# A decoder layer on one core: the first norm's weight from the common load, the first row block in two transfers, four warm-up products in place of five

## The chip, the core and the metric

The kernel runs on one core of one Trainium2 chip. A core has a matrix engine (TensorE, PE in the profile, with its weight loads shown apart as PEld), three engines for elementwise work (VectorE = DVE, ScalarE = ACT, GpSimd = POOL), an engine that mostly starts transfers (SyncE = SP), and 16 DMA engines that all queues share. TensorE multiplies operands that lie in SBUF and writes to PSUM; the input tensors lie in HBM and come in by DMA. The metric is the device time of one execution in microseconds (us); lower is better.

## The reference

One layer of a decoder trunk over 256 tokens of width 1024, in float32:

```python
n = _rmsnorm(x, norm_mix_g)                    # x * rsqrt(mean(x*x) + EPS) * g
z = n @ w_in                                   # conv a, conv gate, q, k, v, index q/k/w, two gates
y_conv = _conformer_conv(c_a, c_g, ...)        # a * sigmoid(gate), 31 taps, layer norm, silu, w_conv_out
y_attn = _dsa_attention(q, k, v, qi, ki, wi) @ w_attn_out
h = x + (g_conv * y_conv + g_attn * y_attn) @ w_mix_out
h = h + _cross_attention(_rmsnorm(h, norm_x_g), _rmsnorm(mem, norm_mem_g), wx_q, wx_kv, wx_o)
h = h + square(relu(_rmsnorm(h, norm_ffn_g) @ w_ff1)) @ w_ff2
return _rmsnorm(h, norm_final_g)
```

The change touches the first line only: how `x` and `norm_mix_g` reach the chip, and what TensorE does until they are there.

## The kernel before

The order of the work is written out by hand (`tc.manual_schedule()`): each engine runs its instructions in the order in which the code issues them, and waits at an instruction for the semaphores that this instruction needs. Weights come as chunks of 1 MB (`wst`, called `raw0`, `raw1`, ... in the order of `STREAM`); the function `load(parts)` starts one chunk from SP, in so many transfers. A weight is split on the chip into a high and a low float32r part (`hi` on ACT, `lo` on DVE), and a product with the normed input (`n_p`, also split in two) is done in three parts.

The first chunk, `raw0` (key `("conv", 0)`, in `WHOLE`), is different: it isn't split but used as plain float32 and multiplied with `xg`, which is `x` transposed and multiplied by the norm's weight `g`, before the norm's root is known. Its two halves are the gate (`ps_conv00`, named `ps_first` in the code) and the value (`ps_conv01`) of the first 128 channels. All of this is the start of the program:

- Lines 501 to 513, transfers: `g_first` (128 x 8 numbers, 4 KB) is started from ACT's queue; the two row blocks of `x` (128 rows x 1024 columns, 512 KB each, into the tile `x_rm`) from SP's queue; `vec`, the load of all small vectors (36 KB, among them `g_mix`, the same numbers as `g_first`), from POOL's queue. Then SP starts `raw0` and `raw1` in two transfers each, `raw2` in one, `cw` (the taps of the convolution) and `raw3`.
- Lines 514 to 533: DVE makes a tile of zeros, POOL an identity matrix, ACT loads its function table, and TensorE runs the warm-up products (`ps_warm`) on the zeros; their result is not used.
- Lines 562 to 587: TensorE transposes the 2 x 8 blocks of 128 x 128 of `x_rm` into four PSUM tiles `pt_n` (row block 0 first, columns 0 to 7, then row block 1). ACT squares row block 0 and half of row block 1 and sums them, DVE squares the other half, POOL raises the mean to the power -1/2 (`rs_n`). ACT (six columns) and DVE (two) write `xg` = `pt_n` times the weight.
- Lines 590 to 609: TensorE starts the products of `raw0` with `xg` for two columns (`first_products(range(2))`), spreads `rs_n` over the partitions (`ps_rsb_n`), and goes on with the products; meanwhile DVE and ACT make `n_p`.

Each DMA has a semaphore out of a ring of eight for the transfers of SP and ACT (`DMAHW0` to `DMAHW7`, handed out in the order in which the code starts the transfers); before the ring comes round, the next transfer with the same semaphore waits for the one before it. `vec` has `DMASW0`, of POOL's own ring.

Of the kernel before, what the change touches and what calls it, by code (L numbers as in the profile page):

```python
# [8 lines left out]
F32 = mybir.dt.float32  # L9
F32R = mybir.dt.float32r  # L10
BF16 = mybir.dt.bfloat16
AF = mybir.ActivationFunctionType
ALU = mybir.AluOpType
# [3 lines left out]
P = 128  # L17
D = 1024
S = 256
KT = D // P  # L20
# [101 lines left out]
def block_kernel(ctx, tc, x, xt, mem, memt, wst, wki, vecs, convw, gout, out):  # L122
    nc = tc.nc
    ctx.enter_context(tc.manual_schedule())
    pe = Counted(nc.tensor, pe_price)
    dve = Counted(nc.vector, dve_price)
    act = nc.scalar.activation

    cst = ctx.enter_context(tc.tile_pool(name="cst", bufs=1))
# [8 lines left out]
    def t8(name, dt=F32, shape=(P, KT, S)):  # L138
        return big.tile(list(shape), dt, tag="t8", bufs=12, name=name)
# [19 lines left out]
    def ps_aux(name):  # L159
        return bank("aux", 2, name)  # L160
# [337 lines left out]
        return lambda ct, ps: copy_out(dst[:, ct, :], ps)  # L498


    g_first = cst.tile([P, KT], F32, name="g_first")
    nc.scalar.dma_start(g_first, vecs[:, 5 * KT : 6 * KT])
    x_rm = t8("x_rm", F32, (P, 2, D))
    for rb in range(2):
        nc.sync.dma_start(x_rm[:, rb, :], x[rb * P : (rb + 1) * P, :])
    vec = cst.tile([P, 72], F32, name="vec")
    nc.gpsimd.dma_start(vec, vecs)
    bgc, bga, cvb, lng, lnb, g_mix, g_mem, g_x, g_ffn = (vec[:, 8 * j : 8 * j + 8] for j in range(9))
# [20 lines left out]
    nc.scalar.activation(half, half, AF.Sigmoid, bias=0.0, scale=0.0)  # L529
    nc.gpsimd.memset(half, -0.5)  # L530
    ps = ps_aux("ps_warm")
    for j in range(5):
        nc.tensor.matmul(ps, zero_r[:, :P], zero_r, start=True, stop=True)


# [30 lines left out]
    xg = t8("xg")  # L566
# [15 lines left out]
    for kt in range(KT):  # L582
        src = ptn[kt // 2][:, (kt % 2) * S : (kt % 2) * S + S]
        if kt in (4, 6):
            dve.tensor_scalar(xg[:, kt, :], src, g_first[:, kt : kt + 1], None, ALU.mult)
        else:
            act(xg[:, kt, :], src, AF.Copy, scale=g_first[:, kt : kt + 1])


    first = whole["conv", 0]  # L590
# [903 lines left out]
    for c in range(JOINED):  # L1494
        hidden.append(Hidden(c + 2))
        x, later = hidden[c], hidden[c + 2]
# [135 lines left out]
```

## Time and profile before

| | us |
|---|---|
| median of 3 runs | 497.66 |
| lowest, highest run | 497.27, 502.79 |
| the profiled execution | 497.16 |
| its span, from the first to the last instruction | 495.0 |
| TensorE (PE) busy | 487.3 |
| VectorE (DVE) busy | 460.5 |
| ScalarE (ACT) busy | 378.4 |
| GpSimd (POOL) busy | 50.6 |

The span is what the trace covers; 497.16 - 495.0 = 2.16 us of the same execution lie outside it. TensorE's line is nearly full from the second 40th of the span to the 39th, so what a stage costs is what it does to TensorE's start, its gaps and its end. The part of the trace that the change touches is the first 8 us of 495; in the timeline's rows the first number is the start in us from the start of the span, the second the duration of the whole group, and the bracket names the idle time ahead of it and what ended it.

### The profile page before, as it was taken

The numbers are of one execution on the slowest core, as the hardware profiler recorded it, in microseconds if no ns is written. First come the engines' busy times: TensorE is split into PE (matmuls) and PEld (weight loads), VectorE is DVE, ScalarE is ACT, GpSimd is POOL, SyncE is SP. The second block draws the span as 40 slices with busy tenths as digits, with TensorE's granted clock in tenths as the row PEclk, the third lists the DMA queues.
The fourth block names the chain that finished last, engine by engine and source line by source line (L and its number), as shares of the span: only waits on it lengthen the run. The fifth ranks groups of instructions, "written<-read, shape, count | busy, mean of one in ns | idle before, by whom it ended". The sixth has DMA issues, their size and how long they took to land.

```text
span 495.0 us, 7793 instructions
## 1 busy us (share of the span) xinstructions
PE 487.3 (98%) x2832; PEld 429.2 (87%) x2832; DVE 460.5 (93%) x828; ACT 378.4 (76%) x678; POOL 50.6 (10%) x67
## 2 busy tenths in 40 slices
PE   8999999999999999999999999999999999999995
PEld 7888888888888889888889999988998888888884
DVE  4999999999999989989988987899999999999986
ACT  5778879999887786767846558687777878888852
POOL 2002212221111211000000000000010101121000
PEclk9999999999999999999999999999999999999999
DMA  8958676989887977354645552866979879999802
GB/s 318 354 215 276 180 190 198 304 245 253 277 219 223 246 176 213 115 171 175 250 169 183 209 204 87 290 189 138 253 274 292 237 242 262 294 333 314 256 9 85
DMA packets 33430, 110.36 MB, mean 223 GB/s; under 512 B 11104, under 2 KB 13408, under 8 KB 24432
## 3 DMA queue, kind: packets, MB, share of 16 engines
q1 hardware_dynamic: 24416, 93.03, 54.4%
q0 software_dynamic: 8688, 16.64, 17.2%
q8 instruction: 22, 0.36, 0.3%
q10 hardware_dynamic: 288, 0.20, 0.1%
q14 instruction: 16, 0.13, 0.1%
HBM read 99.29 MB, written 1.05 MB: 203 GB/s over the span
## 4 chain that ended last, share of the span: by engine, by line
PE 97%; DVE 1%; issue 0%; ACT 0%; DVEq 0%
PE ps_f L87 18%; PE ps_p L87 15%; PE ps_conv L87 9%; PE ps_co L87 5%; PE ps_mix L87 5%; PE ps_ao L87 5%; PE ps_k L87 5%; PE ps_ga L87 5%; PE ps_gc L87 5%; PE ps_q L87 5%; PE ps_v L87 4%; PE ps_xo L87 3%; PE ps_xq L87 2%; PE ps_xk L87 2%; PE ps_qi L87 2%; PE ps_xv L87 2%
## 5 line engine op out<-in xcount | busy, mean ns | idle before, releaser
L87 DVE TENSOR_TENSOR lo<-raw,hi 128x1024 fp32r<-128x1024 f32 x133 | 161.3, 1215 | 2.5 <-ACT hi L315 2.2
L315 ACT ACTIVATE hi<-raw 128x1024 fp32r<-128x1024 f32 x133 | 138.5, 1048 | 6.2 <-DMA raw<-in_wst_dram 6.1
L87 PE MATMUL ps_f<-ff_p,hi 128*128 128x512 f32 (+1 forms) x320 | 72.4, 347 | 0.0
L87 PEld LDWEIGHTS ps_f<-ff_p,hi 128*128 128x128 f32 x320 | 56.2, 189 | 8.2 <-ACT ft L1344 0.3
L87 DVE SCALAR_TENSOR_TENSOR acc<-u,cw,acc 128x241 f32<-128x241 f32 (+23 forms) x142 | 58.5, 465 | 0.1
L87 PE MATMUL ps_f<-ff_p,lo 128*128 128x256 f32 x256 | 46.8, 282 | 0.0
L87 PEld LDWEIGHTS ps_f<-ff_p,lo 128*128 128x128 f32 x256 | 39.3, 191 | 1.8
L715 POOL DMA_DIRECT2D acc<-products x25 | 21.7, 880 | 124.2 <-ACT products L714 59.5
L87 PE MATMUL ps_conv<-n_p,hi 128*128 128x512 f32 x112 | 29.2, 397 | 0.0
L87 PEld LDWEIGHTS ps_conv<-n_p,hi 128*128 128x128 f32 x112 | 20.4, 188 | 4.4 <-issue 0.3
L714 ACT ACTIVATE products<-u,cw 128x243 f32<-128x243 f32 (+19 forms) x50 | 22.1, 492 | 0.0
L293 ACT ACTIVATE inner<-sums 128x1024 fp32r<-128x1024 f32 x13 | 13.8, 1060 | 10.5 <-DVE sums L87 10.5
L87 DVE TENSOR_TENSOR ft<-ft 128x128 f32<-128x128 f32 (+2 forms) x49 | 19.4, 397 | 1.1 <-ACT ft L1344 0.6
L683 ACT ACTIVATE ring<-u,cw 128x236 f32<-128x236 f32 (+10 forms) x44 | 20.2, 480 | 0.0
L87 PE MATMUL ps_p<-outer,fs 128*128 128x512 f32 x78 | 20.1, 393 | 0.0
L87 PE MATMUL ps_v<-hi,n_p 128*128 128x512 f32 x64 | 19.9, 389 | 0.0
L87 PE MATMUL ps_p<-inner,fs 128*128 128x512 f32 x78 | 19.8, 389 | 0.0
L87 PE MATMUL ps_co<-u_p,hi 128*128 128x512 f32 (+1 forms) x80 | 19.3, 350 | 0.0
L87 PE MATMUL ps_mix<-mix_p,hi 128*128 128x512 f32 (+1 forms) x80 | 19.2, 349 | 0.0
L87 PE MATMUL ps_k<-n_p,hi 128*128 128x512 f32 x64 | 17.4, 403 | 0.0
L87 PE MATMUL ps_q<-n_p,hi 128*128 128x512 f32 x64 | 17.3, 402 | 0.0
L87 PEld LDWEIGHTS ps_p<-inner,fs 128*128 128x128 f32 x78 | 14.6, 188 | 3.0
(445 smaller groups left out, 1215.0 us busy)
## 6 DMA issues: line engine op xcount, KB each, us to landing
raw<-in_wst_dram SPq DMA_DIRECT2D x67, 1024.0 KB, 5.7
raw<-in_wst_dram SPq DMA_DIRECT2D x28, 512.0 KB, 6.7
sums<-in_wst_dram POOLq DMA_DIRECT2D x15, 512.0 KB, 8.0
acc<-products POOLq DMA_DIRECT2D x25, 256.0 KB, 5.5
x_rm<-in_x_dram SPq DMA_DIRECT2D x2, 512.0 KB, 4.0
mem_rm<-in_mem_dram SPq DMA_DIRECT2D x1, 1024.0 KB, 7.6
mem_t<-in_memt_dram SPq DMA_DIRECT2D x1, 1024.0 KB, 9.6
h_t<-in_xt_dram SPq DMA_DIRECT2D x1, 1024.0 KB, 7.0
```

The source lines that it names most:

```text
L87: return fn(*args, **kwargs)
L293: act(hi, src, AF.Copy)
L315: act(hi, raw[:, ns], AF.Copy)
L683: act(dst[:, t, :], u[:, 4 * g + t, : S - s], AF.Copy, scale=cw[:, 4 * g + t, TAPS - 1 - s : TAPS - s])
L714: act(prod[:, a, s:], u[:, t, : S - s], AF.Copy, scale=cw[:, t, TAPS - 1 - s : TAPS - s])
L715: nc.gpsimd.dma_start(acc[:, ts, :], prod, accum_op=ALU.add)
```

## The change

`g_first` and its transfer go away, and `xg` is made with `g_mix`, a slice of `vec`. Row block 0 of `x` comes in two transfers, columns 0 to 511 and 512 to 1023; row block 1 in one, as before. One of the five warm-up products is left out. Nothing that is computed changes.

```diff
-    g_first = cst.tile([P, KT], F32, name="g_first")
-    nc.scalar.dma_start(g_first, vecs[:, 5 * KT : 6 * KT])
     x_rm = t8("x_rm", F32, (P, 2, D))
-    for rb in range(2):
-        nc.sync.dma_start(x_rm[:, rb, :], x[rb * P : (rb + 1) * P, :])
+    for rb, cols in ((0, slice(0, 512)), (0, slice(512, D)), (1, slice(0, D))):
+        nc.sync.dma_start(x_rm[:, rb, cols], x[rb * P : (rb + 1) * P, cols])
     vec = cst.tile([P, 72], F32, name="vec")
     nc.gpsimd.dma_start(vec, vecs)
...
     ps = ps_aux("ps_warm")
-    for j in range(5):
+    for j in range(4):
         nc.tensor.matmul(ps, zero_r[:, :P], zero_r, start=True, stop=True)
...
         if kt in (4, 6):
-            dve.tensor_scalar(xg[:, kt, :], src, g_first[:, kt : kt + 1], None, ALU.mult)
+            dve.tensor_scalar(xg[:, kt, :], src, g_mix[:, kt : kt + 1], None, ALU.mult)
         else:
-            act(xg[:, kt, :], src, AF.Copy, scale=g_first[:, kt : kt + 1])
+            act(xg[:, kt, :], src, AF.Copy, scale=g_mix[:, kt : kt + 1])
```

The instructions keep their order on every engine; what moves is what each waits for. On TensorE, at the start of the program, before the change (a row is one instruction or several alike; in brackets the semaphores that it waits for):

```order
L533 MATMUL ps_warm<-zero_r 128x512 x4
L87 MATMUL pt_n_128<-ident,x_rm 128x128 [waits DMAHW1_49,Pool_49]
L87 MATMUL pt_n_128<-ident,x_rm 128x128
L87 MATMUL pt_n_129<-ident,x_rm 128x128 x2
L87 MATMUL pt_n_130<-ident,x_rm 128x128 x2
L87 MATMUL pt_n_131<-ident,x_rm 128x128 x2
L87 MATMUL pt_n_128<-ident,x_rm 128x128 [waits DMAHW2_49]
```

And after it, at the same place:

```order
L531 MATMUL ps_warm<-zero_r 128x512 x3
L87 MATMUL pt_n_126<-ident,x_rm 128x128 [waits DMAHW0_49,Pool_49]
L87 MATMUL pt_n_126<-ident,x_rm 128x128
L87 MATMUL pt_n_127<-ident,x_rm 128x128 x2
L87 MATMUL pt_n_128<-ident,x_rm 128x128 [waits DMAHW1_49]
L87 MATMUL pt_n_128<-ident,x_rm 128x128
L87 MATMUL pt_n_129<-ident,x_rm 128x128 x2
L87 MATMUL pt_n_126<-ident,x_rm 128x128 [waits DMAHW2_49]
```

The first four transposes now wait for the first half of row block 0 alone, the fifth for the second half, the ninth for row block 1 as before; the first product of `raw0` still waits for that chunk's first half (`DMAHW3`) and for `xg`.

On SP, the transfers before the change:

```order
L505 DMA x_rm<-in_x_dram 128x1024 x2
L184 DMA raw_89<-in_wst_dram 128x1024 x2
L184 DMA raw_92<-in_wst_dram 128x1024 x2
L184 DMA raw_95<-in_wst_dram 128x2048
L512 DMA cw<-in_convw_dram 128x248 [waits DMAHW0_49]
L184 DMA raw_98<-in_wst_dram 128x2048 [waits DMAHW1_49]
```

And after it:

```order
L503 DMA x_rm<-in_x_dram 128x512 x2
L503 DMA x_rm<-in_x_dram 128x1024
L184 DMA raw_88<-in_wst_dram 128x1024 x2
L184 DMA raw_91<-in_wst_dram 128x1024 x2
L184 DMA raw_94<-in_wst_dram 128x2048
L510 DMA cw<-in_convw_dram 128x248 [waits DMAHW0_49]
L184 DMA raw_97<-in_wst_dram 128x2048 [waits DMAHW1_49]
```

SP starts one transfer more ahead of all the weights. `cw` waited for `g_first` (`DMAHW0` before) and now waits for the first half of row block 0; `raw3` waited for row block 0 and now waits for its second half.

On ACT, before the change:

```order
L502 DMA g_first<-in_vecs_dram 128x8
L529 ACT_TABLE_LOAD
L529 ACTIVATE half<-half 128x2 [waits Pool_49]
L570 ACTIVATE junk_full,ss_n<-x_rm 128x1024 [waits DMAHW1_49]
L576 ACTIVATE junk_half,ss_n<-x_rm 128x512 [waits DMAHW2_49]
L587 ACTIVATE xg<-pt_n_128,g_first 128x256 [waits DMAHW0_49,PE_49]
```

And after it:

```order
L527 ACT_TABLE_LOAD
L527 ACTIVATE half<-half 128x2 [waits Pool_49]
L568 ACTIVATE junk_full,ss_n<-x_rm 128x1024 [waits DMAHW1_49,DMAHW0_49]
L574 ACTIVATE junk_half,ss_n<-x_rm 128x512 [waits DMAHW2_49]
L585 ACTIVATE xg<-pt_n_126,vec 128x256 [waits DMASW0_49,PE_49]
```

The start of `g_first`'s transfer is gone from ACT, and the first `xg` waits for `vec`, POOL's transfer, in the place of `g_first`.

## The prediction, made before the changed kernel ran

> **What bounds the kernel now.** I read the page first: the engines' busy time and the chain that ended last.
>
> ```profile
> PE 487.3 (98%) x2832; PEld 429.2 (87%) x2832; DVE 460.5 (93%) x828; ACT 378.4 (76%) x678; POOL 50.6 (10%) x67
> ...
> PE 97%; DVE 1%; issue 0%; ACT 0%; DVEq 0%
> ```
>
> TensorE is the bound: 487.3 of 495.0 us, and 97% of the chain. The change can move the end only by moving TensorE's work near the start. So the second view is the chain over the first 20 us (start, duration, what):
>
> ```profile
> 1.43 0.44 DVE zero_r L517
> ...
> 1.91 2.50 PE ps_warm L533 x5
> 4.41 3.62 PE pt_n L87 x16
> 8.03 0.90 PE ps_conv L87 x4
> 8.94 0.22 PE ps_rsb_n L87 x2
> 9.15 10.98 PE ps_conv L87 x57
> ```
>
> This reads as if TensorE were never without work after 1.91 us: warm-up, transposes, products. By it one warm-up product less, half a us of the 2.50, would be a gain of that half. But a chain names what came last by the profile, and a busy bar can end just when a transfer lands. So the third view is the DMA issues of short stretches, which give for one transfer the time from its start to its landing (last column, us), and the fourth SP's timeline with those starts.
>
> ```profile
> x_rm<-in_x_dram SPq DMA_DIRECT2D x1, 512.0 KB, 3.5
> ...
> x_rm<-in_x_dram SPq DMA_DIRECT2D x1, 512.0 KB, 4.4
> ...
> raw<-in_wst_dram SPq DMA_DIRECT2D x1, 512.0 KB, 6.0
> ...
> vec<-in_vecs_dram POOLq DMA_DIRECT2D x1, 36.0 KB, 4.6
> ```
>
> ```profile
> 0.74 0.86 SPq L505 DMA_DIRECT2D x_rm<-in_x_dram  x2
> 1.18 0.42 SPq L505 DMA_DIRECT2D x_rm<-in_x_dram  x1
> 1.28 0.71 POOL L507 DMA_DIRECT2D vec<-in_vecs_dram  x1 [0.83 <-POOLq L1623]
> 1.64 2.49 SPq L184 DMA_DIRECT2D raw<-in_wst_dram  x5
> 4.50 0.33 SPq L512 DMA_DIRECT2D cw<-in_convw_dram  x1
> ```
>
> Row block 0 landed at 0.74 + 3.5 = 4.24 us, row block 1 at 1.18 + 4.4 = 5.58, `vec` at 1.28 + 4.6 = 5.88, the first half of `raw0` at 1.64 + 6.0 = 7.64. Against these stands TensorE's timeline:
>
> ```profile
> 3.78 0.63 PE L533 MATMUL ps_warm<-zero_r 128*128 128x512 f32 x1
> 4.37 0.72 PEld L87 LDWEIGHTS pt_n<-ident,x_rm 128*128 128x128 f32 x4 [0.68 <-issue]
> 4.40 3.63 PE L87 MATMUL pt_n<-ident,x_rm 128*128 128x128 f32 x16
> ...
> 7.42 0.23 PEld L87 LDWEIGHTS pt_n<-ident,x_rm 128*128 128x128 f32 x1
> 7.76 0.23 PEld L87 LDWEIGHTS ps_conv<-xg,raw 128*128 128x128 f32 x1
> ```
>
> Two things are to be seen. The first transpose loads at 4.37, 0.13 us after row block 0 landed, so it waited for the row block, not for the last warm-up product. And the first product of `raw0` loads at 7.76, 0.12 us after that chunk's first half landed at 7.64. The transposes stand (3.63 - 0.42) / 15 = 0.214 us apart (0.42 is one of them), so the next instruction could have loaded at 7.42 + 0.21 = 7.63. TensorE's readiness and the chunk's landing meet within 0.02 us. From there on the products follow each other, and the chain shows nothing but TensorE: **the landing of the first half of `raw0` is the second floor under everything behind it**, and making TensorE ready sooner can't lift it.
>
> **The change, part by part.**
>
> *One warm-up product less.* TensorE is free for the first transpose at 3.78, where the fifth product started, instead of at the fifth's end; five products started within 3.78 - 1.91 us, 0.47 apart.
>
> *The row block in two.* When does the first half land? The busy time by stretch shows what the DMA engines moved (last column, GB/s):
>
> ```profile
> 1.70:2.30 0.60, 0.39 (x1) 0.39 (x2) 0.16 (x1) 0.60 (x1) 0.53 (x3) 1.00 0.91 205
> 2.30:2.70 0.40, 0.40 (x2) 0.30 (x2) 0.00 (x0) 0.19 (x2) 0.40 (x3) 1.00 0.13 51
> 2.70:3.30 0.60, 0.60 (x3) 0.47 (x2) 0.00 (x0) 0.17 (x1) 0.23 (x4) 1.00 0.89 351
> 3.30:3.90 0.60, 0.60 (x3) 0.33 (x1) 0.00 (x0) 0.00 (x0) 0.00 (x0) 1.00 1.11 421
> ...
> 138.60:139.00 0.40, 0.40 (x3) 0.33 (x2) 0.40 (x1) 0.40 (x1) 0.40 (x1) 1.00 0.00 0
> ```
>
> 0.6 us at 205, 0.4 at 51 and 0.6 at 351 GB/s are 0.12 + 0.02 + 0.21 = 0.35 MB by 3.30. Half a block, 0.26 MB, is through at 3.04; the whole, 0.52 MB, at 3.70, and it landed 0.54 later. So the first half should land near 3.04 + 0.54 = 3.6, ahead of 3.78. The transposes then start at about 3.8, 0.57 us sooner. Four of them take 0.85; the second half, due at about 4.3, is there.
>
> Row block 1 is next. Eight transposes end at 3.8 + 1.71 = 5.51, but the block lands at 5.58, and with the 0.11 us from landing to load (0.13 and 0.12 above) the ninth loads at 5.69. Before, it loaded at 7.42 - 7 x 0.214 = 5.92. Of 0.57 us are left 0.23. The transposes end at 5.69 + 1.71 = 7.40, and the first product waits for `raw0` until 7.64 + 0.11 = 7.75, as before. Nothing is left. What is late next is thus the weight transfer.
>
> *Do the landings move?* The bytes stay. The two terms come from packets, in the DMA rows of three stretches of 0.30 us (queue, packets, MB, share of 16 engines):
>
> ```profile
> q1 hardware_dynamic: 31, 0.13, 102.7%
> q10 hardware_dynamic: 29, 0.00, 5.4%
> ...
> q1 hardware_dynamic: 59, 0.12, 104.4%
> ```
>
> A 4 KB packet took 1.027 x 16 x 0.30 / 31 = 0.159 us, a 2 KB one (59 of them, in the output's stage) 0.085, one of `g_first` 0.009. Row block 0 in 2 KB rows costs each engine 8 x (2 x 0.085 - 0.159) = 0.09 us more; without `g_first`, 128 packets and 16 for its semaphore, each engine saves 9 x 0.009 = 0.08. They cancel: 7.64 stays.
>
> Both ends: at the low end, the pause at 2.30 to 2.70 (51 GB/s) comes from `g_first`'s packets and goes with them, which would bring the stream forward by 0.4 x (400 - 51) / 400 = 0.35, with the 0.08 altogether 0.43 us. I don't take it, because the last row of that fence shows the same pause, at 0 GB/s, 0.6 us after a transfer began at 138 us, with no small transfer beside it. At the high end, SP's extra start (0.42 us, the row at 1.18) delays each later start and each landing in full: +0.42 and +0.09, 0.5 us. I don't take it either: time to landing grows from 3.5 to 4.4 to 6.0 along the queue, so the transfers wait behind bytes, not for their start. I take 0.
>
> *`vec` for `g_first`.* It lands at 5.88. The first `xg` is wanted before the product at 7.75, and takes 0.48:
>
> ```profile
> 6.81 1.57 ACT L587 ACTIVATE xg<-pt_n,g_first 128x256 f32<-128x256 f32 x4 [0.44 <-PE pt_n L87]
> 6.89 0.72 POOL L538 TENSOR_TENSOR rs_n<-ss_n,half 128x2 f32<-128x2 f32 x1 [3.84 <-DVE ss_n L87]
> ```
>
> Four `xg` take 1.57 us, or 0.39 apart; even if ACT began only at 7.27 the first product would not wait, so the cover is 7.27 - 5.88 = 1.39 us. Beyond it each us costs one. The two `xg` of DVE and the power (`rs_n`, ready at 7.61 and used at 8.56 or so) come later still.
>
> *The queues.* ACT loses one start, ahead of its table load, which nobody waits for. `cw` started at 4.50; SP now reaches it at 1.64 + 2.49 + 0.42 = 4.55, when its semaphore and that of `raw3` behind it have gone up (by about 4.3). Both transfers stand behind the 4 MB of `x` and three chunks, so 0.05 us costs nothing.
>
> *The sum:* 0 for the end, with -0.43 and +0.5 as its bounds. The profiled execution, 497.16 us (span 495.0 and 2.16 around it), is 0.50 below the median of 497.66.
>
> **The clock.** TensorE ran at half its clock there, which the page's clock line doesn't show. The same kind of transpose, before and after about 7.8 us (min/median/max ns):
>
> ```profile
> L87 PEld LDWEIGHTS pt_n<-ident,x_rm x16: 183/231/231, 4.4 to 7.4; 128*128 128x128 f32 x16
> L87 PE MATMUL pt_n<-ident,x_rm x16: 404/421/447, 4.4 to 7.6; 128*128 128x128 f32 x16
> ...
> L87 PEld LDWEIGHTS ps_rsb_n<-ident,rs_n x2: 137/137/137, 8.6 to 8.8; 128*128 128x128 f32 x2
> L87 PE MATMUL ps_rsb_n<-ident,rs_n x2: 272/272/273, 8.8 to 8.9; 128*128 128x128 f32 x2
> ```
>
> Two of them stand 0.214 us apart before and start 0.11 apart after (0.22 us of chain for two). So a saving at half clock is worth half if the clock rises at a fixed time. It also means that what makes the clock rise matters. The Trainium skill, "TensorE: Matmul & The Clock Gate", Part 4, says that transposes don't count as busy for the clock; Part 1 says it rises after about 3.4 us of sustained work. By the first, the change removes a fifth of what counts. The trace leans against it: between the last warm-up product and 7.8 us there were 16 transposes and nothing else, and the clock rose right then.
>
> **The rivals.**
>
> *A, the forecast:* the weight transfer holds the first product at 7.75. Chance 0.70. The runs lie at 497.27 and 497.66, the profiled one at 497.16; the middle between the median 497.66 and their mean 497.36 is 497.5.
>
> *B, the start-up pause goes with `g_first`:* the earlier start of TensorE then finds its data, up to -0.43: 497.07 from 497.5. For it: small packets stand between all large ones in the second stretch. Against it: the pause at 138.6 us. Chance 0.10.
>
> *C, the clock rises later.* TensorE has about 0.2 us of holes at the ninth transpose and 0.3 at the first product, and one product less. If only products count, the missing 0.47 us is made up by products at half clock: +0.2. If the rise is put off by as long as the half-clock stretch lasted (1.91 to 7.8, 5.9 us), the products of that time take twice as long: +2.95. The middle is +1.6, or 499.1. Against it: what was said of the transposes. Chance 0.10. By the page's window alone, 3.4 us at half clock, the estimate would be +1.7.
>
> *D, the later starts reach the landings:* +0.5, or 498.0, by the high end above. Chance 0.05.
>
> *E, slower by `vec`:* one place, the wait of the first `xg`. It decides from a landing at 7.27 on. POOL's loads in the full stream take longer than 4.6 us:
>
> ```profile
> sums<-in_wst_dram POOLq DMA_DIRECT2D x15, 512.0 KB, 8.0
> ```
>
> With 8.0, `vec` would land at 9.28 and the first product load near 9.8, 2.0 us later: 499.5. Against it: the same transfer at the same time was there at 5.88. Chance 0.05. C, D and E are the cases that end slower than before; none by 2%, which here is 10 us.
>
> **How the numbers follow.** 497.5 us is A. Below, B's end at half chance and A's own spread of runs (0.35 to either side of 497.5) reach 496.9. Above, D and the lower half of C reach 498.6. Left out are C's upper half (0.05), E (0.05) and a median that falls on a disturbed run like 502.79 (0.05 or so): together under 0.2. So 496.9 to 498.6. About 2% is what a measurement of this kernel is held to tell from no change; no case reaches it: faster 0.01, same 0.97, slower 0.02.
>
> **What would show it.** Right: first transpose near 3.8 instead of 4.37, ninth near 5.7 instead of 5.92, a hole of 0.3 us and then the first `ps_conv` load at 7.75 +- 0.1, `ps_rsb_n` behind it at the short 137 ns, `raw`'s first landing at 7.64 (5.6 us after a start near 2.06), span 495.0 +- 0.5. Wrong: that load below 7.5 (B), above 8.1 with the landing (D) or with `vec` (E), or `ps_rsb_n` and the first products at 231 ns and over (C).

## The result: 0.7% slower, and the profile after

| | before | after |
|---|---|---|
| median of 22 runs, us | 497.22 | 500.98 |
| lowest, highest run | 496.92, 502.79 | 498.68, 502.22 |
| the profiled execution | 497.16 | 502.22 |
| its span | 495.0 | 500.1 |

The ratio of the times is 1.0071, with a 95% interval of 1.0057 to 1.0084: a loss of 3.8 us by the medians, under 2%, but outside the range that was predicted. The profiled execution of after is the slowest of its 22, 5.06 us above the profiled one of before; what follows is read from it, and a median execution loses less.

The page of after, busy time and chain shares by engine, stands against the two lines that the prediction began with:

```profile
PE 489.1 (98%) x2831; PEld 430.3 (86%) x2831; DVE 460.7 (92%) x828; ACT 379.4 (76%) x678; POOL 50.8 (10%) x67
...
PE 96%; DMA 2%; DVE 1%; issue 0%; SPq 0%; ACT 0%; DVEq 0%
```

TensorE is still the bound, but a DMA now holds 2% of the chain, where none stood before. The chain over the first 22 us (start, duration, what) says which:

```profile
1.64 0.43 SPq L503
2.07 0.04 issue
2.11 7.83 DMA raw<-in_wst_dram
9.95 0.14 issue
10.08 2.05 PE ps_conv L87 x4
12.13 0.43 PE ps_rsb_n L87 x2
12.56 9.56 PE ps_conv L87 x35
```

SP starts three pieces of `x`, so `raw0` starts at 2.11 and not at 1.64, and its first half lands at 9.95 and not at 7.64. The landing is 2.31 us late for a start that is 0.47 late. The DMA issues of after, the first two from the stretch 1.50 to 2.00 us and the last two from 2.00 to 2.40 (last column: us from start to landing):

```profile
x_rm<-in_x_dram SPq DMA_DIRECT2D x1, 256.0 KB, 3.2
vec<-in_vecs_dram POOLq DMA_DIRECT2D x1, 36.0 KB, 5.9
...
x_rm<-in_x_dram SPq DMA_DIRECT2D x1, 512.0 KB, 6.8
raw<-in_wst_dram SPq DMA_DIRECT2D x1, 512.0 KB, 7.8
```

The second half of row block 0 started at 1.18 and landed at about 4.3; row block 1 started at 1.64 and landed at 8.4, 2.8 us later than before (5.58). What TensorE did meanwhile, its timeline and its waits (us in total, times, longest):

```profile
2.50 1.48 PE L531 MATMUL ps_warm<-zero_r 128*128 128x512 f32 x3
3.78 1.91 PE L87 MATMUL pt_n<-ident,x_rm 128*128 128x128 f32 x8
8.44 0.77 PE L87 MATMUL pt_n<-ident,x_rm 128*128 128x128 f32 x5 [2.74 <-DMA x_rm<-in_x_dram]
```

```profile
PE pt_n L87 <- DMA x_rm<-in_x_dram: 2.7, 1, 2.7
...
PE ps_conv L87 <- DMA raw<-in_wst_dram: 0.6, 1, 0.6
```

The first eight transposes run as forecast, from 3.78 on; then TensorE stands idle for 2.74 us until row block 1 is there. The chain names `raw0` alone, because it follows the landing that came last; but row block 1 by itself already holds the transposes until 8.44 + 1.10 = 9.54 (1.10 us for all eight), so both late landings delay the first product.

The clock is the other half. Stretches of after (busy time of each engine, then PEclk, DMA share, GB/s), and the second kind of row the prediction asked for, the weight loads of `ps_rsb_n`:

```profile
6.10:9.30 3.20, 0.86 (x8) 0.86 (x8) 0.70 (x2) 0.89 (x3) 0.00 (x0) 1.00 0.87 309
9.50:16.20 6.70, 6.15 (x17) 4.88 (x17) 4.37 (x10) 3.94 (x10) 0.98 (x2) 0.50 1.02 418
16.30:20.00 3.70, 3.70 (x19) 3.26 (x18) 3.62 (x6) 3.70 (x6) 0.00 (x0) 1.00 0.33 137
```

```profile
L87 PEld LDWEIGHTS ps_rsb_n<-ident,rs_n x2: 231/231/231, 11.5 to 11.9; 128*128 128x128 f32 x2
```

231 ns instead of 137: half the clock. The trace's record of the granted clock has it rise at 6.03, fall at 9.44 and rise again at 16.27, after steps of 3.41 and 6.83 us. Before, it rose at 7.88 and stayed. So the products from 10.08 to 16.27 ran at half clock, which costs about 6.19 / 2 = 3.1 us; the first product was 10.08 - 7.84 = 2.24 us late. Together 5.3, and the first product with `n_p` came at 20.15 instead of 14.85, 5.3 later. That accounts for the difference of the two spans, 5.1.

Last, the transfers. The stretch of the start-up pause in after, and a later one, and below the later one in before:

```profile
2.30:2.70 0.40, 0.40 (x2) 0.30 (x2) 0.00 (x0) 0.04 (x1) 0.40 (x3) 1.00 1.05 394
3.20:6.80 3.60, 2.49 (x10) 1.75 (x9) 0.00 (x0) 1.15 (x2) 0.00 (x0) 1.00 0.68 181
```

```profile
3.20:6.80 3.60, 3.60 (x15) 2.82 (x15) 0.86 (x3) 1.87 (x4) 0.00 (x0) 1.00 1.02 351
```

The pause at 2.3 us (51 GB/s before) is gone, but from 3.2 to 6.8 the engines moved 181 GB/s instead of 351. For each of these transfers the trace marks 16 arrivals, as many as there are DMA engines; call each a share. The transfer has landed with the last one. The arrivals of the first half of `raw0` (us, sorted):

```
before  7.10 7.11 7.12 7.14 7.15 7.16 7.25 7.26 7.27 7.30 7.32 7.37 7.53 7.54 7.58 7.65
after   7.05 7.18 7.22 7.25 7.48 7.56 7.64 8.51 9.64 9.66 9.76 9.77 9.80 9.88 9.91 9.95
```

Seven shares of after came about as early as before, one was held up by about 1 us and eight by more than 2: the shares have come apart.

### The profile page after: what moved, and what is told of

The parts are those of the page before. It is cut to its first block, busy times and chain, and to the rows that moved or that the text cites. A ratio compares the mean times of both kernels' runs of the same rounds, so it can differ in the third digit from the quotient of the medians.

```text
span 500.1 us, 7792 instructions
## 1 busy us (share of the span) xinstructions
PE 489.1 (98%) x2831; PEld 430.3 (86%) x2831; DVE 460.7 (92%) x828; ACT 379.4 (76%) x678; POOL 50.8 (10%) x67
## 4 chain that ended last, share of the span: by engine, by line
PE 96%; DMA 2%; DVE 1%; issue 0%; SPq 0%; ACT 0%; DVEq 0%
PE ps_f L87 18%; PE ps_p L87 15%; PE ps_conv L87 10%; PE ps_co L87 5%; PE ps_mix L87 4%; PE ps_ao L87 4%; PE ps_k L87 4%; PE ps_ga L87 4%; PE ps_gc L87 4%; PE ps_q L87 4%; PE ps_v L87 4%; PE ps_xo L87 3%; PE ps_xq L87 2%; PE ps_xk L87 2%; PE ps_qi L87 2%; PE ps_xv L87 2%
## 5 line engine op out<-in xcount | busy, mean ns | idle before, releaser
L293 ACT ACTIVATE inner<-sums 128x1024 fp32r<-128x1024 f32 x13 | 13.8, 1061 | 11.0 <-DVE sums L87 10.9
```

The source lines that it names most:

```text
L293: act(hi, src, AF.Copy)
```

## The experiments

Two questions stand behind the loss: what disturbs the transfers, and what TensorE's hole costs. For the first there were several theories, tried in turn, which bear letters in the expectations. S: the third transfer of `x` itself makes row block 1 late. C: one warm-up product less lowers the clock. V: POOL's `vec`, now the first reader of `vecs`, collides with row block 1. P: the 2 KB pieces. T: the first access to the weights' tensor costs a pause. N: a transfer lands out of proportion late when SP starts it later. Q: a later start costs only its own length. The kernel before ran beside each, with medians of 497.2 or so.

| run | median us | ratio, 95% interval | `raw0` starts | its first half lands | packets over 0.6 us |
|---|---|---|---|---|---|
| after | 500.98 | 1.0071 [1.0057, 1.0084] | 2.11 | 9.95 | 6 |
| g_first kept | 500.35 | 1.0085 [1.0049, 1.0120] | 2.11 | 8.81 | 2 |
| split alone | 500.12 | 1.0052 [1.0037, 1.0067] | 2.12 | 8.61 | 5 |
| g_first's removal alone | 498.34 | 1.0028 [1.0013, 1.0044] | 1.65 | 8.97 | 8 |
| four warm-up products alone | 497.29 | 1.0036 [0.9994, 1.0078] | 1.64 | 7.66 | 0 |
| hole filled | 498.69 | 1.0032 [1.0019, 1.0044] | 2.12 | 10.20 | 6 |
| vec from ACT | 499.99 | 1.0060 [1.0042, 1.0078] | 2.11 | 9.27 | 12 |
| split, vec late | 500.14 | 1.0057 [1.0035, 1.0080] | 2.11 | 9.26 | 13 |
| before, vec late | 496.85 | 0.9986 [0.9977, 0.9996] | 1.64 | 7.65 | 0 |
| split by rows | 499.77 | 1.0058 [1.0042, 1.0074] | 2.63 | 9.32 | 9 |
| second half from ACT | 499.50 | 1.0051 [1.0036, 1.0067] | 1.64 | 7.68 | 0 |
| split, early touch | 500.70 | 1.0093 [1.0055, 1.0130] | 2.11 | 9.07 | 14 |
| vec late, early touch | 497.39 | 1.0009 [0.9991, 1.0027] | 1.64 | 7.63 | 0 |
| small load between | 498.29 | 1.0022 [1.0003, 1.0041] | 2.11 | 9.52 | 1 |
| small load before `raw0` | 498.30 | 1.0006 [0.9982, 1.0029] | 2.12 | 8.25 | 7 |
| small load first | 498.46 | 1.0004 [0.9954, 1.0054] | 2.11 | 8.36 | 2 |
| vec late, four warm-up products | 496.94 | 0.9992 [0.9977, 1.0007] | 1.64 | 7.56 | 0 |

Landings and packets are of the one profiled execution each, the medians of 4 to 10 runs (after: 22); the last column counts 4 KB packets from 2.3 to 10 us that took over 0.6 us. The profiled execution of g_first's removal took 505.05, far above its median.

**The three parts of the change, apart.** After with `g_first` back; before with the split alone; before without `g_first` alone; before with four warm-up products alone.

```diff
# split alone, against before
-    for rb in range(2):
-        nc.sync.dma_start(x_rm[:, rb, :], x[rb * P : (rb + 1) * P, :])
+    for rb, cols in ((0, slice(0, 512)), (0, slice(512, D)), (1, slice(0, D))):
+        nc.sync.dma_start(x_rm[:, rb, cols], x[rb * P : (rb + 1) * P, cols])
# g_first's removal alone, against before (and its use by g_mix)
-    g_first = cst.tile([P, KT], F32, name="g_first")
-    nc.scalar.dma_start(g_first, vecs[:, 5 * KT : 6 * KT])
# four warm-up products alone, against before
-    for j in range(5):
+    for j in range(4):
```

> The changed kernel with g_first's own 4 KB load put back (xg uses it again); the row block stays in two transfers and the warm-up at four. Three theories. V (the small vectors: without g_first, the 36 KB load of vec is the first to read that tensor, at 3.4 us, and holds up half of the DMA engines ahead of row block 1): about 497.2 us, row block 1 landing by 5.7 us. S (the split: one transfer more on SP's queue leaves row block 1 late): about 501, landing near 8.4. C (the clock: one warm-up product less): about 500, with the clock falling back although row block 1 is in time.

> The kernel before with the split of row block 0 alone (g_first and five warm-up products kept). V: 497.2 us, as before. S: 500 to 501, row block 1 landing near 8.4. C: 497.2. If only split and missing g_first together do it: 497.2.

> The kernel before without g_first alone (xg uses the slice of vec; row block 0 in one transfer, five warm-up products). V: 499 to 501 us, a transfer behind vec landing 2 to 3 us late. S and C: 497.2. If only split and missing g_first together do it: about 497.2, or a part of the loss.

> The kernel before with four warm-up products in place of five, nothing else. V and S: 497.2 us, since the first transpose waits for row block 0 at 4.24 us anyway. C: 499 or more, with the full clock granted one stretch later than 7.8 us.

The split alone costs 2.9 us of the 3.8, and with `g_first` kept after hardly gets better (500.35, its runs from 499.45 to 505.28). TensorE's timeline of the split alone:

```profile
6.51 1.09 PE L87 MATMUL pt_n<-ident,x_rm 128*128 128x128 f32 x8 [0.58 <-DMA x_rm<-in_x_dram]
8.75 0.51 PE L87 MATMUL ps_conv<-xg,raw 128*128 128x256 f32 x1 [1.14 <-ACT xg L587]
```

The second bracket names ACT, but the first half of `raw0` landed at 8.61, 0.14 us ahead of the product, as in after. Row block 1 landed at 6.47 here and at 6.92 with `g_first` kept, between what V (5.7) and S (8.4) had expected; in after and in the filled hole below, both with the split and without `g_first`, it was 8.39 and 8.56. So part of row block 1's lateness seems to come with `g_first`'s removal; each of these is one execution.

The removal of `g_first` alone costs 1.1 by the medians, with nine of ten runs spread from 497.34 to 500.61. The warm-up product costs nothing that can be seen: 497.29, with 1 inside the interval, and the clock rose at 8.20, beside 7.88 before; C falls. TensorE's timeline of that run shows why:

```profile
4.52 3.65 PE L87 MATMUL pt_n<-ident,x_rm 128*128 128x128 f32 x16 [0.53 <-DMA x_rm<-in_x_dram]
```

The half us that the fifth product took is idle time now, ended by the row block's landing. So the split is the main part of the loss. Added up, the three parts alone cost 2.9 + 1.1 + 0.1 = 4.1 us, beside 3.8 together.

**Is it `vec`?** After with `vec` started first of all on ACT's queue; and the split with `g_first` kept, four warm-up products and `vec` started on POOL only after the power (at 8.20 us); and before with `vec` late in the same way (at 7.56).

```diff
# vec from ACT, against after
-    nc.gpsimd.dma_start(vec, vecs)
+    nc.scalar.dma_start(vec, vecs)    # ahead of the loop over x
# vec late: the line nc.gpsimd.dma_start(vec, vecs) stands behind POOL's power
```

> The changed kernel with one difference: the load of all vectors (36 KB) starts from ACT's queue at 0.74 us, where g_first's stood, in place of POOL's. Two theories on why row block 1 lands late. V (POOL's transfer of vec gets its turn at the boundary between the halves of row block 0 and row block 1, and holds up the engines there): 497.0 to 497.3 us, row block 1 by 5.7 us and the first half of raw0 by 7.7. S (the third transfer of x itself): 500 or more, row block 1 after 6.4.

> The run e1 (g_first kept, row block 0 in two transfers, four warm-up products) with vec's load started from POOL after the power of the first norm (about 7.6 us) instead of at 1.28; nothing before 17 us needs it then. V: 497.2 us or less, row block 1 by 5.7 us. S: 500.3, as e1, row block 1 after 6.4.

> The kernel before with vec's load started from POOL after the power of the first norm (about 7.6 us), nothing else. V: the first half of raw0 lands up to 0.3 us sooner than 7.65, and the time is 497.2 or 0.1 to 0.2 less, since the transposes end at 7.63 anyway. S: 497.2, no landing moves.

The DMA issues of the first of these, from the stretches 0.60 to 1.10 and 2.00 to 2.40:

```profile
vec<-in_vecs_dram ACTq DMA_DIRECT2D x1, 36.0 KB, 3.3
...
raw<-in_wst_dram SPq DMA_DIRECT2D x1, 512.0 KB, 7.2
```

`vec` is there after 3.3 us, by about 4.0, and `raw0` is still late, 9.27. With `vec` out of the way altogether it lands at 9.26. Theory V falls as the main cause: the times stay at 500. Without a split, `vec` late gains 0.4 us (0.9986), the only version whose interval lies below 1. The landing of `raw0` did not move there (7.65), and no run shows where the gain comes from.

**What the hole costs.** After, with eight unused products of zeros behind row block 0's transposes, so that TensorE has work until row block 1 lands.

```diff
+        if rb == 0:
+            for j in range(8):
+                nc.tensor.matmul(ps, zero_r[:, :P], zero_r, start=True, stop=True)
```

> The changed kernel with eight more products on zeros behind the transposes of row block 0, so that TensorE has work in most of the hole while row block 1 is late; no load is touched. If the clock falls because of the hole: the full clock stays from its first grant on, the products of raw0 run 0.22 us apart from the first, and the median is 1 to 3 us under the changed kernel's 501 (498 to 500). If the lateness of the transfers is all: 501 or, by the eight products, up to 1.7 more.

It gave 498.69 (498.41 to 499.54), 2.3 us under after. Its chain:

```profile
10.20 0.14 issue
10.34 1.10 PE ps_conv L87 x4
11.44 0.22 PE ps_rsb_n L87 x2
```

Here `raw0` landed even later than in after (10.20), but four products took 1.10 us instead of 2.05: the clock rose at 7.03 and stayed. Nothing else in the start was changed, so of after's 3.8 us about 2.3 are the clock's, lost by the hole; the other 1.5, the lateness, are what is left by subtraction.

That a hole lowers the clock is not certain in every execution, as the other traces show. In the split alone (idle for 0.58 and 1.14 us), the split with the early touch (2.25) and `g_first`'s removal alone (1.89), the clock rose, as in after, and fell again for 3.41 us (in after for 6.83). With `g_first` kept, `vec` from ACT, the split by rows, the second half from ACT and the small load between, it rose only at 10.6 to 13.8 us. In before, in four warm-up products alone and in the three versions with `vec` late and no split it had risen at 6.9 to 8.2 and stayed, and with the small load first at 8.61. But in the split with `vec` late it rose at 6.77 and stayed through 1.80 us of idle time, and with the small load before `raw0` it rose at 6.07 and stayed through 1.19. Which of the three happens, these traces don't settle.

**Is it the 2 KB pieces, or the first access?** Three kernels on the base of split, `vec` late (`g_first` kept, four warm-up products): the row block cut into two of 64 rows (4 KB packets); its second half from ACT's queue, so that SP's starts are as in before; and an unused 4 KB load of `raw0`'s first columns, early on ACT's queue. And that early load with before, `vec` late.

```diff
# split by rows
+    for lo, hi in ((0, 64), (64, P)):
+        nc.sync.dma_start(x_rm[lo:hi, 0, :], x[lo:hi, :])
...
# second half from ACT
+    nc.sync.dma_start(x_rm[:, 0, :512], x[:P, :512])
+    nc.scalar.dma_start(x_rm[:, 0, 512:], x[:P, 512:])
...
# early touch
+    nc.scalar.dma_start(touch, wst[INDEX[("conv", 0)]][:, :KT])
```

> The run e6 (g_first kept, four warm-up products, vec late) with row block 0 cut by rows instead of columns: two transfers of 64 rows of 4 KB each, so as many transfers as e6 but the packets of the kernel before. P (the 2 KB pieces of rows are what makes the later transfers late): 496.9 us, row block 1 by 5.7 and the first half of raw0 by 7.7. N (the number of transfers ahead of the weights): 500, as e6.

> The run e6 with the second half of row block 0 started from ACT's queue behind g_first, so that SP starts row block 1 and all weights as early as in the kernel before. N (SP's starts): 497 us. P (2 KB pieces): 500. If the two queues' pieces get in each other's way: 500 as well, with row block 0 whole later than 4.3.

> The run e6 with one more 4 KB load from ACT's queue behind g_first, of 128 x 8 numbers out of raw0's rows, which nothing uses. T (what is late is the first access to the weights' tensor, which a tiny early load pays ahead of time): the first half of raw0 by 7.2 us, 497 us or less. N and P: 500, as e6, raw0's first half after 8.6.

> The run e8 (the kernel before with vec late) with that same unused 4 KB load of raw0's rows. T: the dip of the transfers at 5.6 to 6.8 us goes, the first half of raw0 lands near 7.1 instead of 7.65, and the time is 496.7 to 496.9, since the transposes end near 7.6 anyway. Otherwise as e8, 496.85, or slower by what the extra load costs (0.1).

Rows of 4 KB land as late as those of 2 KB, though here SP's starts were later still (2.63), so P is weakened rather than excluded by this run alone. The early touch helps in neither (500.70; 497.39, 0.5 above `vec` late without it): T falls. The second half from ACT gave the clearest answer, though from one execution; its DMA issues, the last row from 1.60 to 1.80:

```profile
x_rm<-in_x_dram SPq DMA_DIRECT2D x1, 512.0 KB, 4.8
...
x_rm<-in_x_dram ACTq DMA_DIRECT2D x1, 256.0 KB, 5.0
...
raw<-in_wst_dram SPq DMA_DIRECT2D x1, 512.0 KB, 6.0
```

With SP's start of `raw0` back at 1.64, it lands after 6.0 us, at 7.68, on time, in spite of the split and its 2 KB pieces (three of these took 0.68 to 0.88 us; the table counts only 4 KB packets). The time is no better (499.50) for the reason that the expectation named third: row block 0 is late. Its second half landed at 6.20, with loads from two queues under way at once, TensorE waited 1.2 us for `x`, its first product came at 8.86 and the clock rose at 10.64.

**A later start without a split.** The kernel before with one unused 4 KB load on SP, between the row blocks, ahead of `raw0`, or first of all; and last, the best version with four warm-up products.

```diff
+    spare = cst.tile([P, KT], F32, name="spare")
     nc.sync.dma_start(x_rm[:, 0, :], x[0:P, :])
+    nc.sync.dma_start(spare, x[0:P, 0:KT])
     nc.sync.dma_start(x_rm[:, 1, :], x[P : 2 * P, :])
```

> The kernel before, with one unused 4 KB load (128 rows x 8 columns of x) started on SP between the two row blocks; nothing is split, g_first and five warm-up products stay. Row block 1 and both halves of raw0 start about 0.42 us later, row block 0 as before. Theory N (a later start on SP lands out of proportion late): row block 1 lands 0.8 us or more later than 5.62, raw0's first half at 8.6 or later, first product 8.7 or later, time above the kernel before by 1 us or more (498.2 or more). Rival Q (a start costs its own length; it is the split of a row block that disturbs the transfers): row block 1 at 6.0 to 6.1, raw0's first half at 8.0 to 8.1, time +0.2 to +0.5.

> As the last, with the unused 4 KB load after row block 1, so that only raw0 and what is behind it start 0.42 us later. Theory N: row block 1 lands at 5.6 as before, raw0's first half at 8.6 or later, time +1 us or more. Rival Q: raw0's first half at 8.0 to 8.1, time +0.2 to +0.5.

> The kernel before with the unused 4 KB load as SP's first, so that row block 0 and all behind it start 0.42 us later. Theory N in its form 'the later a transfer is started after the others' first packets the worse': all landings are later by 0.4 to 0.6 alone (4.7, 6.1, 8.1), time +0.3 to +0.6. If N holds in the form 'any start beyond 1.64 us on SP is punished': raw0's first half at 8.6 or later, time +1 us or more. Rival Q: +0.3 to +0.5.

> The kernel before with vec's load started later on POOL (as in the run with vec late alone) and four warm-up products instead of five. Both theories: the landings stay at 4.2, 5.5 and 7.65, the first product near 7.8, time as with vec late alone, 496.6 to 497.2. If it is above 497.4, the fifth product is worth something.

Wherever the extra start stands, the time is 498.3 to 498.5, 1.1 to 1.3 us above the kernel before by the medians. The intervals of the second and third include 1, because runs of 500 and more fall into both sides; but nine of the second's ten runs lie between 498.01 and 498.74, none of either lies below 497.94, and 25 of the 31 runs of before in this batch lie at 497.70 or lower. On the landing Q came nearer where the small load stands ahead of `raw0` or first: 8.25 and 8.36, 0.6 and 0.7 late. With the small load ahead of `raw0`, row block 1 landed at 6.17 instead of 5.62 although it started at 1.18 as before, which neither theory had expected: in this execution a transfer that was started ahead of the extra start is held up too. The DMA issues and the wait of the second run:

```profile
raw<-in_wst_dram SPq DMA_DIRECT2D x1, 512.0 KB, 6.1
```

```profile
PE ps_conv L87 <- DMA raw<-in_wst_dram: 1.2, 1, 1.2
```

On the time N's bound, +1 or more, held. The first run's profiled execution (500.95, its median 498.29) shows the large form: 15 of 16 shares of row block 1 came in by 6.21, the last at 7.98. So N and Q are both half right: usually the delay is 0.5 to 0.7 us, and now and then one share or several fall back by 2. Nor is the extra start all: the split alone has SP start its transfers at the same times as the small load between (0.74, 1.18, 1.64 and 2.11 or 2.12), and is 1.8 us slower by the medians. The fifth warm-up product is worth nothing here either (496.94 beside 496.85 in another batch).

## Why the prediction was wrong

*The sum that the runs give.* One more start on SP: +1.1 (three kernels without a split). The clock, lost by TensorE's hole: +2.3 (hole filled). Rest: 3.8 - 1.1 - 2.3 = 0.4, within the spread of these medians. The terms come from different kernels and may overlap (in the profiled execution of the small load between, the clock rose only at 11.31), and the 1.1 us of `g_first`'s removal alone have no place in this sum; so it is a working, not a proof. The split alone fits within one execution: its first product came at 8.75, 0.91 late, and the clock was down from 9.02 to 12.43, 3.41 us at half speed, so 1.7 us; together 2.6 of the 2.7 by which its span (497.7) is longer.

*Do the landings move? "I take 0".* This step failed first. The high bound of that place, SP's extra start of 0.42 with 0.09 for the packets, named the place, and was put aside with the argument that the time to landing grows along the queue, so that the transfers wait behind bytes. They don't wait behind bytes alone: the same start cost 0.6 to 0.7 us of landing without a split, and up to 2.3 in after. The bound itself was too low: it let all 16 shares move together, and the extra start alone cost 1.1 us of time. What the runs showed in place of the 0: row block 1 2.8 us late, the first half of `raw0` 2.3 us late, and the end 3.8 us later by the medians.

*The pause at 2.30 to 2.70 was held not to be `g_first`'s.* That failed. In after, without `g_first`, 394 GB/s moved where 51 had; with `g_first`'s removal alone it was 399 from 2.40 to 2.80, beside 83 before. But the low bound, a gain of 0.43, was wrong too: nothing was gained, and `g_first`'s removal alone cost about 1 us. From 3.2 us on, about when `vec`'s packets come (the first at 3.38), the engines move less than before. That the pause goes over to the next reader of `vecs` fits after's windows, but late `vec` didn't cure the split, so it is argued and not shown.

*The hole at the ninth transpose, 0.2 us by the forecast, was 2.74.* This follows from row block 1's landing. TensorE being ready sooner was counted as harmless; with a late landing it lengthens the hole, here by up to the 0.6 us of the earlier start.

*The clock* was held for a rival by itself (C, 0.10), with one product less and two holes of 0.2 and 0.3 us as the cause. Its upper size was near, +2.95 against 2.3. The missing product was not the cause, for four products alone lost nothing. In after it was the hole, but one of 2.74 us, which C did not have; filling it kept the clock. C and D were priced as alternatives where one brings the other about: lateness makes the hole, the hole lowers the clock. Their sum on 497.5, 0.5 + 2.95, would have come to 500.95, next to the measured 500.98. That is luck in the sizes, since the first term measured more and the second less; and no chance was given to the two together.

*On the Trainium skill's rule* that transposes don't count as busy ("TensorE: Matmul & The Clock Gate", Part 4): in before 16 transposes filled the time from 4.40 to the rise at 7.88, and in the run with the small load ahead of `raw0` the clock rose at 6.07, after five products and eight transposes. These traces lean against it for this kind of float32 transpose. The window of about 3.4 us in Part 1 of that page of the Trainium skill agrees: in the first 17 us, every stretch between two changes of the clock is 3.41 or 6.83 us long.

*What came as forecast:* the first transpose at 3.78 (forecast 3.8), the second half of row block 0 at 4.3 (4.3), and the warm-up product worth nothing. `vec` did not decide (E), but by luck: it landed at 7.2, not at 5.88, just short of the 7.27 from which it would have counted, and the late transposes hid it.

*What stays open* is why some shares fall back. The table's last columns bound it. In six kernels whose `raw0` starts at 1.64, no 4 KB packet after 2.3 us took over 0.47 us, and its first half lands at 7.56 to 7.68. In all eleven where it starts at 2.11 or later, after among them, between 1 and 14 packets took 0.6 to 2.0 us, all started from 3.2 to 6.5 us. But a late start is not needed: in the profiled execution of `g_first`'s removal alone (505.05 us in all), `raw0` started at 1.65, and still eight packets took 0.6 to 1.0 us and its first half landed at 8.97. What these packets wait for the trace doesn't name, and the tensor's first access, the packet size and `vec` were tried without effect.

## What to carry to other kernels

Where a landing and an engine meet within some hundredths of a us, price a step on the queue as a delay of the transfers around it, and ask how long the engine then stands still: a hole of TensorE near the start costs its own length, and where the clock falls or rises late with it, half of that stretch besides (about 3.1 us in after's profiled execution, 1.7 in that of the split alone, nothing in that of the split with `vec` late). Splitting a load so that the engine starts sooner only helps if the next load is there when the first is used up. Rivals that have one cause belong into one sum.

## What was not expected of the hardware

- One more start of 0.42 us on SP at the head of the program cost 1.1 to 1.3 us of time by the medians, although it carried 4 KB.
- The shares of one transfer can come apart at the start: seven landed by 7.64 us and eight from 9.64 to 9.95.
- The clock can fall right after it rose: up at 6.03, down at 9.44, after a hole of 2.74 us, and up again only 6.83 us later. After 1.80 us of idle time in another version it stayed up.
- The second half of row block 0, 256 KB, took 5.0 us to land from ACT's queue, beside 3.2 from SP's in after.
